# A gain row fetched one group later, and an eviction set behind two weight splits, in a one-layer diffusion block

## The chip, the core and the metric

The kernel runs on one NeuronCore of a Trainium2 chip. Five engines run side by side, each with its own instruction stream: TensorE (PE) multiplies matrices into PSUM; VectorE (DVE) and ScalarE (ACT) work on elements of SBUF and PSUM; GpSimd (POOL) does a few small operations; SyncE (SP) issues most of the DMA transfers, and ACT and POOL issue some. Instructions of one engine start in their order, and engines wait for each other, and for transfers, through semaphores. The metric is the time of one execution in microseconds (us).

## The reference

One layer of a diffusion transformer on 1024 latent tokens and 256 context tokens, width 1024, in float32. With the constants put in, and the parts cut that the change does not touch:

```
sh1, sc1, gt1, sh2, sc2, gt2 = split(silu(c) @ w_mod + b_mod, 6)
h_x = rmsnorm(x, g_pre_mix) * (1 + sc1) + sh1          # the same for the context, with c_ctx
u, q, k, v = split(h @ w_in)                           # latent; of the context only k and v are used
attn = softmax(q k^T / 8 + bias, neighbourhood + all context keys) v
x = x + gt1 * rmsnorm(concat(pool(u), attn) @ w_out, g_post_mix)
h = rmsnorm(x, g_pre_mlp) * (1 + sc2) + sh2
y = square(relu(h @ w_mlp_in)) @ w_mlp_out             # 1024 -> 4096 -> 1024
x = x + gt2 * rmsnorm(y, g_post_mlp)
```

Two quantities matter below. The keys and values of the 256 context tokens come from `w_in`, early in the kernel. The second gate `gt2` is multiplied with the row `g_post_mlp`, and the product scales the MLP's result at the very end.

## The kernel before, in words

**Split products.** Every large product is made of three matmuls: both operands are split into a rounded high part and the rest (`split`, `high_low`), and high x high, high x low and low x high are summed in PSUM (`three`, lines 197 to 200, where most of TensorE's records lie). ACT makes the high part (`high_part`, line 146, or 148 with a factor) and DVE the low part (`low_part`, line 152 or 154). A weight of 128x1024 thus needs one load, one ACT and one DVE instruction before its matmuls can start, the low part being wanted by the second matmul.

**The buffers.** `wraw` has 4 buffers for loaded weights, `whl` has 8 for split ones (so four weights), `act` has 33 pages of 128x1024. They are taken in turn; a new tile waits until the last reader of the old one in that buffer is done.

**The beginning.** Up to line 699 (`startup`) the order on all five engines is the written one. `context_keys(j, ks)` sums the keys of the context in four tiles `pkc0` to `pkc3`, and after the last step of each, ACT copies the PSUM bank into `kc` (line 692). The tiles 2 and 3 come last, each with 24 matmuls over the four split weights `wk0` to `wk3`. Then `difference(0)` runs on DVE, and line 698 splits the four weights of the values, `wv0` to `wv3`, in order, into the buffers that `wk0` to `wk3` leave. The first product with them is `pvc`, the values of the context (line 736), followed by `pv`, those of the latent tokens. The copied keys are read in the attention, much later.

**The MLP's first half** works on 16 blocks of 256 hidden units (`block_pair`), with a fast matrix scheme of seven products (P1 to P7) in place of eight. Its results are stored to DRAM through ACT's DMA queue (`keep`, line 1584). With the last block, the stores are put off and issued at its end by `flush`; the last but one of these is `hdA<-c`. In the last block, the items 0 to 2 of the second half are already prepared (`ahead()` is then `prepare`).

**The MLP's second half** (from line 1808) again holds PE, ACT, DVE and SP to the written order. Its temporary pool `tmp3` is opened where that of the first half, `tmp2`, is closed, so its first tiles lie where the first half's parts lay. The work is a list of items (product, group), each with a load of weights (line 1710, `b`), a load of a stored hidden part (line 1726, `hrA` or `hrS`) and two splits. The first product is P1 with 8 groups, the bank set `pyx`. `group(ps, name, g)` first calls `prepare()`, which sets up the item three places ahead, and then issues the 24 matmuls of group g: so group 0 prepares item 3, group 1 prepares item 4, and so on. The hidden parts of items 0 to 4 of P1 go into `wraw`, later ones into `tmp3`. P1 is followed by P6 and P2 in turns, then P7 and P5, and P4 and P3.

**The second gate.** Its sum over the layer's input, `accb`, is complete in the first half. `mod_gain` loads the row `g_post_mlp` (`gp2`) in four small transfers from SP into the tile `gpb` of `tmp3` (line 243). `mod_gate` sums `accb` over the partitions with four matmul calls (line 236) into the bank `pgb` and multiplies by `gpb` on DVE (line 247). `mod_out` stores the product with four DMAs of POOL (line 253), and in the middle of P6 `gate_page` loads it again, spread over all partitions, as the page that scales the result's rows (line 1847).

Of the kernel before, what the change touches and what calls it, by code (L numbers as in the profile page):

```python
# [11 lines left out]
F32 = mybir.dt.float32  # L12
# [6 lines left out]
P = 128  # L19
D = 1024  # L20
KT = D // P
# [59 lines left out]
def hybrid_block(ctx, tc, x, ctx_in, w_mod, b_mod, gp1, gp2, w_in, pool_w, rpb, w_out, w1, w2, vectors,  # L81
                 mask, edge, out):
    nc = tc.nc
# [97 lines left out]
    def high_low(name, raw, factor=1.0):  # L181
        hi = whl.tile([P, 1024], F32R, tag="hl", name=f"{name}h")
        lo = whl.tile([P, 1024], F32R, tag="hl", name=f"{name}l")
        split(raw, hi, lo, factor)
        return hi, lo
# [7 lines left out]
    def wk(w, k, lo, c, n):  # L193
        return w[k // 2][lo][:, (k % 2) * 512 + c : (k % 2) * 512 + c + n]


    def three(ps, ahi, alo, bhi, blo, first, last, more=False):
        nc.tensor.matmul(ps, ahi, bhi, start=first, stop=False, skip_group_check=more)  # L198
        nc.tensor.matmul(ps, ahi, blo, start=False, stop=False, skip_group_check=more)  # L199
        nc.tensor.matmul(ps, alo, bhi, start=False, stop=last, skip_group_check=more)  # L200
# [39 lines left out]
    def mod_gain(gp, g):  # L240
        quarters = gp.rearrange("(c o f) -> c o f", c=4, o=1)
        for c in range(4):
            nc.sync.dma_start(g[32 * c : 32 * c + 32, :], quarters[c].to_broadcast([32, 256]))
        return g

    def mod_gate(name, acc, g, bank):
        nc.vector.tensor_tensor(acc[:, :256], mod_sums_of(name, acc, bank), g, mul)


    def mod_out(name, acc):  # L250
        gates[name] = dram.tile([1, D], F32, tag=f"g{name}", name=f"g{name}")
        for c in range(4):
            nc.gpsimd.dma_start(gates[name][:, c * 256 : (c + 1) * 256], acc[32 * c : 32 * c + 1, :256])
# [17 lines left out]
    with tc.tile_pool(name="ps1", bufs=6, space=PSUM) as ps1, tc.tile_pool(name="tmp1", bufs=3) as tmp:  # L271

        def bank(name):
            if name[:2] == "pm" or name in ("pxt1_0", "pxt0_2", "pxt1_7", "pct2", "pct3"):
                return lasting(name)
            return ps1.tile([P, 512], F32, tag="mm", name=name)
# [163 lines left out]
        wgt = []  # L440
# [62 lines left out]
        def in_weights(name, raw, kk):  # L503
            return high_low(f"{name}{kk}", raw[kk], 1.0 if kk < 2 else -1.0)
# [62 lines left out]
        hc, wgt = [], []  # L567
# [10 lines left out]
        page_of, raw_v = [], []  # L578
# [66 lines left out]
        def pooled(g, up):  # L645
            w = WINDOWS[g]
            lo, hi = w // 2, w - 1 - w // 2

            bufs = [page(f"sa{g}"), page(f"sb{g}")]
            cur, span, i = up, 1, 0  # L650
            while span < w:
                nxt = bufs[i % 2]
                i += 1
                n = SEQ - 2 * span + 1
                nc.vector.tensor_tensor(nxt[:, :n], cur[:, :n], cur[:, span : span + n], add)
                cur, span = nxt, 2 * span

            ed = tmp.tile([P, 16], F32, tag="ed", name=f"ed{g}", bufs=2)
            nc.vector.reduce_sum(ed[:, 0:1], up[:, 0 : hi + 1], axis=mybir.AxisListType.X)
            for q in range(1, lo):  # L660
                nc.vector.tensor_tensor(ed[:, q : q + 1], ed[:, q - 1 : q], up[:, hi + q : hi + q + 1], add)
            if hi:
                nc.vector.reduce_sum(ed[:, 7 + hi : 8 + hi], up[:, SEQ - 1 - lo : SEQ], axis=mybir.AxisListType.X)
            for q in range(hi - 2, -1, -1):
                t = SEQ - hi + q
                nc.vector.tensor_tensor(ed[:, 8 + q : 9 + q], ed[:, 9 + q : 10 + q], up[:, t - lo : t - lo + 1], add)
            dp = bufs[i % 2]
            nc.vector.scalar_tensor_tensor(dp[:, lo : SEQ - hi], cur[:, : SEQ - w + 1], 1.0 / w,
                                           up[:, lo : SEQ - hi], mul, sub)
            nc.vector.tensor_tensor(ed[:, :lo], ed[:, :lo], edg[:, g, :lo], mul)  # L670
            nc.vector.tensor_tensor(dp[:, :lo], ed[:, :lo], up[:, :lo], sub)
            if hi:
                nc.vector.tensor_tensor(ed[:, 8 : 8 + hi], ed[:, 8 : 8 + hi], edg[:, g, 8 : 8 + hi], mul)
                nc.vector.tensor_tensor(dp[:, SEQ - hi :], ed[:, 8 : 8 + hi], up[:, SEQ - hi :], sub)
            return dp
# [3 lines left out]
        def difference(g):  # L679
            differences[g] = pooled(g, up[g]).rearrange("p (r m c) -> p m r c", r=QR, m=NM)  # L680

        kcp = page("kcT")
        kc = kcp.rearrange("p (j t) -> p j t", j=4)
        pkc = {}

        def context_keys(j, ks):
            if j not in pkc:
                pkc[j] = bank(f"pkc{j}")[:, :CTX]
            for k in ks:
                three(pkc[j], wk(wgt, k, 0, j * P, P), wk(wgt, k, 1, j * P, P), *hc[k], k == 0, k == KT - 1)  # L690
            if k == KT - 1:
                nc.scalar.copy(kc[:, j], pkc[j])

        for js, ks in (((0, 1), range(6)), ((0, 1), (6, 7)), ((2, 3), range(KT))):
            for j in js:
                context_keys(j, ks)
        difference(0)
        wgt = [in_weights("wv", raw_v, kk) for kk in range(KT // 2)]
        startup.close()


# [220 lines left out]
        with in_order(ET.PE, ET.Pool, ET.Activation, ET.DVE, ET.SP) as pooling:  # L922
            banks = {of: [bank(f"p{of}{j}") for j in range(2)] for of in "KQ"}
            use(-1)
            for step, (n, of, j) in enumerate([(n, of, j) for n, of in products for j in range(2)]):
                half_product(n, of, j, banks[of])
                use(step)
                if step in (5, 9, 17):
                    name = {5: "S1", 9: "S4", 17: "S3"}[step]
# [4 lines left out]
                if step in (7, 11):  # L934
                    name = {7: "S4", 11: "S3"}[step]
# [13 lines left out]
    with (  # L949
# [195 lines left out]
        with in_order(ET.PE, ET.Activation, ET.DVE, ET.SP) as projected:  # L1145
# [7 lines left out]
            for i in range(N + 4):  # L1153
# [12 lines left out]
                if i > 3:  # L1166
                    weighed(i - 4)
                    if i % 8 == 3:
                        j = i // 8 - 1
# [3 lines left out]
                if i == 0:  # L1173
                    gain = mod_gain(gp1, att.tile([P, 256], F32, tag="gp", name="gpa"))
# [10 lines left out]
                if 8 < i < N and i % 8 == 7:  # L1185
                    j = i // 8 - 1
# [63 lines left out]
    with tc.tile_pool(name="ps2", bufs=6, space=PSUM) as ps2:  # L1250
# [6 lines left out]
      with ExitStack() as tmp2:  # L1257
        tmp = tmp2.enter_context(tc.tile_pool(name="tmp2", bufs=4))
# [549 lines left out]
        with tc.issue_after(first[ET.PE]), in_order(ET.PE, ET.Activation, ET.DVE, ET.SP):  # L1808
# [5 lines left out]
            tmp = tmp2.enter_context(tc.tile_pool(name="tmp3", bufs=4))  # L1814

            def four(name):
                return [bank(f"{name}_{t}") for t in range(4)]
# [13 lines left out]
            def group(ps, name, g, more=False, last=False):  # L1831
                prepare()
                for t in range(4):
                    token_sums(ps, t, [made.pop((name, g)) if t == 3 else made[name, g]], g == 0 and not more,
                               last or g == NG - 1, more)
# [32 lines left out]


            pg = bank("pgb")  # L1870
            gain = mod_gain(gp2, tmp.tile([P, 256], F32, tag="gp", name="gpb", bufs=1))
            x = four("pyx")
            for g in range(NG):
                if g == 2:
                    mod_gate("b", acc_b[-1], gain, lambda name: pg)
                    mod_out("b", acc_b[-1])
                group(x, "P1", g)
# [84 lines left out]
```

## Time and profile before

| What | Value |
|---|---|
| time, median of 3 runs | 1043.54 us (1043.27 to 1044.52) |
| the profiled execution's own time | 1043.7 us |
| its span, first to last instruction | 1041.9 us |
| TensorE busy | 1021.6 us, 98% of the span |
| DVE busy | 755.9 us, 73% |
| ACT busy | 544.0 us, 52% |
| DMA | 221.63 MB, mean 213 GB/s |
| granted TensorE clock, mean | 0.995 |

How to read the rows that follow. A row of the order in time has: start in us, duration in us, engine, line of the kernel, operation, the tile written, an arrow, the tiles read, the shapes, and in brackets how long the engine had stood before it and for whom. Numbers of tiles are partly left out: `b_3h` is the high part of `b11_3`, `c` is `c21_15`. PEld is TensorE's loading of weights, and SPq, ACTq are the issuing of DMAs. A row of waits has: who waited, for whom, us in total, times, longest. A table by stages has for each window its length, then busy us (and instructions) of PE, PEld, DVE, ACT and POOL, the granted TensorE clock as a share of full, the DMA share and GB/s. A matmul's listed duration is longer than its distance to the next one, since they are pipelined.

### The profile page before, as it was taken

Reading aid. Unit: us, or ns where it says so; the run is one execution under the profiler, and the core shown is the slowest. Engines: PE = TensorE matmul, PEld = TensorE weight load, DVE = VectorE, ACT = ScalarE, POOL = GpSimd, SP = SyncE. Lnnn points to the kernel's source line nnn. Section 1 sums busy time; section 2 is a strip of 40 time slices with the busy share of each in tenths; the row PEclk is TensorE's granted clock in tenths of the full one; section 3 lists DMA queues with packets and bytes.
Section 4 is the critical chain, followed back from the end, with each engine's and each line's share of the span. In section 5 each row is a group of like instructions: output and inputs, shape, how many; then the busy total and the mean of one; then the engine's idle time right before and its main releaser. Section 6 shows DMA issues by size and latency. Waiting matters only on the chain.

```text
span 1041.9 us, 15640 instructions
## 1 busy us (share of the span) xinstructions
PE 1021.6 (98%) x5814; PEld 838.0 (80%) x5814; DVE 755.9 (73%) x1183; ACT 544.0 (52%) x941; POOL 108.3 (10%) x163
## 2 busy tenths in 40 slices
PE   8999999999999999999999999999799999999997
PEld 7788888878877888888888888888588888888885
DVE  5587856878986687879988888755476666547586
ACT  7582254328886657776555554545453334334431
POOL 3011021143311321310000000000000000000001
PEclk9999999999999999999999999999899999999999
DMA  9999699641337966886786667343877666555456
GB/s 345 323 261 325 232 241 303 205 101 43 72 95 190 216 179 194 276 206 204 256 263 210 210 199 239 137 151 132 337 261 282 235 231 223 200 173 194 171 186 207
DMA packets 122908, 221.63 MB, mean 213 GB/s; under 512 B 9424, under 2 KB 55248, under 8 KB 122832
## 3 DMA queue, kind: packets, MB, share of 16 engines
q1 hardware_dynamic: 96608, 170.75, 49.5%
q0 software_dynamic: 9088, 18.92, 9.2%
q10 hardware_dynamic: 17136, 30.97, 8.0%
q8 instruction: 45, 0.74, 0.3%
q14 instruction: 31, 0.25, 0.1%
HBM read 167.63 MB, written 51.92 MB: 211 GB/s over the span
## 4 chain that ended last, share of the span: by engine, by line
PE 92%; ACT 2%; DMA 2%; DVE 2%; issue 1%; SPq 0%; ACTq 0%; DVEq 0%; POOLq 0%
PE pu L449 4%; PE S L977 3%; PE pa L1053 3%; PE pyv L199 3%; PE pyz L199 3%; PE pyv L200 3%; PE pyz L200 3%; PE pyz L198 3%; PE pyv L198 3%; PE phx L198 3%; PE phx L199 3%; PE phx L200 3%; PE phv L198 3%; PE phz L198 3%; PE phv L199 3%; PE phz L199 3%
## 5 line engine op out<-in xcount | busy, mean ns | idle before, releaser
L1000 ACT ACTIVATE sp<-sp,nm 128x640 f32<-128x640 f32 (+1 forms) x64 | 51.4, 803 | 20.0 <-DVE nm L991 19.7
L1563 ACT ACTIVATE c<-c 128x512 f32<-128x512 f32 x48 | 30.3, 632 | 48.1 <-DVE c L1683 24.5
L146 ACT CAST wpS<-S 128x512 fp32r<-128x512 f32 x64 | 38.8, 616 | 28.2 <-PE phv L200 10.1
L198 PE MATMUL phx<-thB,wpA 128*128 128x512 f32 x128 | 50.2, 392 | 0.0
L199 PE MATMUL phx<-tlB,wpA 128*128 128x512 f32 x128 | 49.8, 389 | 0.0
L200 PE MATMUL phx<-thB,wpA 128*128 128x512 f32 x128 | 49.8, 389 | 0.0
L152 DVE TENSOR_TENSOR wpS<-S,wpS 128x512 fp32r<-128x512 f32 x64 | 43.4, 685 | 8.2 <-ACT wpS L146 8.2
L991 DVE CUSTOM_DVE_ANT_0 sp<-S,tab 128x640 f32<-128x640 f32 (+1 forms) x56 | 42.8, 802 | 8.4 <-PE S L977 6.8
L1564 ACT ACTIVATE c<-c 128x512 f32<-128x512 f32 x48 | 30.3, 631 | 14.8 <-DVE sa L1646 12.1
L140 POOL TENSOR_TENSOR ry<-vy,nhalf 128x1 f32<-128x1 f32 x8 | 4.4, 550 | 282.8 <-DVE vy L138 282.8
L198 PEld LDWEIGHTS phx<-thB,wpA 128*128 128x128 f32 x128 | 24.0, 188 | 5.5 <-ACT s L1614 0.5
L977 PE MATMUL S<-kT,q 64*128 64x384 f32 (+1 forms) x128 | 27.8, 495 | 0.3 <-DVE nm L991 0.3
L200 PEld LDWEIGHTS phx<-thB,wpA 128*128 128x128 f32 x128 | 24.0, 188 | 5.1
L199 PEld LDWEIGHTS phx<-tlB,wpA 128*128 128x128 f32 x128 | 24.0, 188 | 4.8
L1053 PE MATMUL pa<-pt,v 128*64 128x128 f32 x352 | 25.9, 279 | 0.8 <-ACT px L1033 0.3
L1038 DVE COPY pt<-T 128x512 f32<-128x512 f32 x32 | 21.9, 686 | 5.5 <-PE T L1019 5.5
L198 PE MATMUL phv<-thT,wpA 128*128 128x512 f32 x64 | 25.0, 391 | 0.0
L198 PE MATMUL phz<-thB,wpS 128*128 128x512 f32 x64 | 25.0, 391 | 0.0
L199 PE MATMUL phv<-tlT,wpA 128*128 128x512 f32 x64 | 24.9, 390 | 0.0
L200 PE MATMUL phz<-thB,wpS 128*128 128x512 f32 x64 | 24.9, 389 | 0.0
L199 PE MATMUL phz<-tlB,wpS 128*128 128x512 f32 x64 | 24.9, 389 | 0.0
L200 PE MATMUL phv<-thT,wpA 128*128 128x512 f32 x64 | 24.9, 389 | 0.0
(1104 smaller groups left out, 3385.1 us busy)
## 6 DMA issues: line engine op xcount, KB each, us to landing
b<-in_w SPq DMA_DIRECT2D x64, 512.0 KB, 4.1
hrS<-hdS SPq DMA_DIRECT2D x32, 512.0 KB, 5.4
hrA<-hdA SPq DMA_DIRECT2D x24, 512.0 KB, 6.4
wm<-in_w_mod SPq DMA_DIRECT2D x16, 512.0 KB, 9.8
wa_0w<-in_w SPq DMA_DIRECT2D x16, 512.0 KB, 4.8
wa_1w<-in_w SPq DMA_DIRECT2D x16, 512.0 KB, 4.3
hdA<-c ACTq DMA_DIRECT2D x32, 256.0 KB, 2.2
hdS<-sa ACTq DMA_DIRECT2D x32, 256.0 KB, 2.4
```

The source lines that it names most:

```text
L146: nc.scalar.copy(hi, src)
L152: nc.vector.tensor_tensor(lo, src, hi.bitcast(F32), sub)
L198: nc.tensor.matmul(ps, ahi, bhi, start=first, stop=False, skip_group_check=more)
L199: nc.tensor.matmul(ps, ahi, blo, start=False, stop=False, skip_group_check=more)
L200: nc.tensor.matmul(ps, alo, bhi, start=False, stop=last, skip_group_check=more)
L449: nc.tensor.matmul(pus[b][j], wk(wgt, k, low, j * P, P), r, start=(k == 0 and n == 0), stop=(k == KT - 1 and n == 2))
L977: nc.tensor.matmul(S[e][:, c0 : c0 + keys.shape[1]], q[hs, cols], keys[hs], start=True, stop=True)
L991: nc.vector.tensor_tensor_reduce(out=to, in0=s, in1=bt, scale=1.0, scalar=BIG, op0=add, op1=ALU.min, accum_out=nm)
L1000: nc.scalar.activation(sp, sp, AF.Exp, bias=least[i, e], scale=-1.0, accum_out=sums[i][:, e : e + 1])
L1053: nc.tensor.matmul(pa[e * HD : (e + 1) * HD, cols], v[:, f : f + HD], turns[i][:, e, c] if c < 4 else fifths[i][:, :, (e + 1) * HD : (e + ...
L1563: nc.scalar.activation(r, src, AF.Relu)
L1564: nc.scalar.activation(r, r, AF.Square)
```

## The change

Two edits. In the beginning, the copy of a context tile's bank into `kc` is taken out of `context_keys` into `context_kept(j)`. For the tiles 0 to 2 it is called where it was. For tile 3 it is called between the split of `wv1` and the split of `wv2`, so that on ACT the order is `wv0h`, `wv1h`, copy, `wv2h`, `wv3h` in place of copy, `wv0h`, `wv1h`, `wv2h`, `wv3h`.

In the MLP's second half, `mod_gain` (the tile `gpb` and its four transfers) is called in the loop over P1's groups, ahead of group 1, in place of ahead of group 0. On SP it thus follows the two loads of the item (P1, 3) and precedes those of (P1, 4). `mod_gate` and `mod_out` are called ahead of group 3 in place of group 2.

```diff
             for k in ks:
                 three(pkc[j], wk(wgt, k, 0, j * P, P), wk(wgt, k, 1, j * P, P), *hc[k], k == 0, k == KT - 1)
-            if k == KT - 1:
-                nc.scalar.copy(kc[:, j], pkc[j])
+
+        def context_kept(j):
+            nc.scalar.copy(kc[:, j], pkc[j])
 
         for js, ks in (((0, 1), range(6)), ((0, 1), (6, 7)), ((2, 3), range(KT))):
             for j in js:
                 context_keys(j, ks)
+                if ks[-1] == KT - 1 and j < 3:
+                    context_kept(j)
         difference(0)
-        wgt = [in_weights("wv", raw_v, kk) for kk in range(KT // 2)]
+        wgt = []
+        for kk in range(KT // 2):
+            wgt.append(in_weights("wv", raw_v, kk))
+            if kk == 1:
+                context_kept(3)
         startup.close()
...
             pg = bank("pgb")
-            gain = mod_gain(gp2, tmp.tile([P, 256], F32, tag="gp", name="gpb", bufs=1))
             x = four("pyx")
             for g in range(NG):
-                if g == 2:
+                if g == 1:
+                    gain = mod_gain(gp2, tmp.tile([P, 256], F32, tag="gp", name="gpb", bufs=1))
+                if g == 3:
                     mod_gate("b", acc_b[-1], gain, lambda name: pg)
                     mod_out("b", acc_b[-1])
                 group(x, "P1", g)
```

## The prediction

> **What bounds the kernel now.** I read the page first: how long the span is, who fills it, and which engine carries the chain that ends last.
>
> ```profile
> span 1041.9 us, 15640 instructions
> PE 1021.6 (98%) x5814; PEld 838.0 (80%) x5814; DVE 755.9 (73%) x1183; ACT 544.0 (52%) x941; POOL 108.3 (10%) x163
> PE 92%; ACT 2%; DMA 2%; DVE 2%; issue 1%; SPq 0%; ACTq 0%; DVEq 0%; POOLq 0%
> ```
>
> TensorE is busy for 98% and carries 92% of the chain, so a change is worth what it gives or takes at the few places where TensorE waits. The second view is therefore the list of waits of TensorE alone, over the whole run, and beside it the longest wait of SP's queue around the largest of them.
>
> ```profile
> PE pyx L198 <- ACT b_3h L146: 5.5, 1, 5.5
> ...
> PE pvc L198 <- ACT wv0h L146: 1.4, 1, 1.4
> ...
> PE pyx L199 <- DVE b_3l L152: 0.7, 1, 0.7
> ```
> ```profile
> SPq L243 <- DMA hdA<-c: 27.4, 1, 27.4
> ```
>
> The reader is to see that two of TensorE's waits lie exactly where the diff is: `pyx` waits for the operands of group 3 of the product P1 (`b_3`), and `pvc` waits for the first weights of the values (`wv0`). SP stood 27.4 us on L243, which is `mod_gain`, until a store at the end of the MLP's first half (`hdA<-c`) had landed. The third view, the order in time on SP, shows what stood behind that wait; ACT and DVE show what came of it; PE shows the price.
>
> ```profile
> 705.51 0.34 SPq L1726 DMA_DIRECT2D hrA<-hdA  x1
> 733.46 1.73 SPq L243 DMA_DIRECT2D gpb<-in_gp  x4
> 735.30 0.38 SPq L1710 DMA_DIRECT2D b<-in_w  x1
> 735.73 0.47 SPq L1726 DMA_DIRECT2D hrA<-hdA  x1
> ```
> ```profile
> 731.08 0.49 ACTq L1584 DMA_DIRECT2D hdS<-sb  x1
> 740.66 1.04 ACT L146 CAST hhA_3h<-hrA 128x1024 fp32r<-128x1024 f32 x1 [10.87 <-DMA hrA<-hdA]
> 741.61 1.04 ACT L146 CAST b_3h<-b 128x1024 fp32r<-128x1024 f32 x1
> ```
> ```profile
> 742.88 1.22 DVE L152 TENSOR_TENSOR b_3l<-b,b_3h 128x1024 fp32r<-128x1024 f32 x1
> ```
> ```profile
> 736.79 0.39 PE L200 MATMUL pyx<-b_2h,hhA_2l 128*128 128x512 f32 x1
> 742.70 0.79 PE L198 MATMUL pyx<-b_3h,hhA_3h 128*128 128x512 f32 x1 [5.52 <-ACT b_3h L146]
> 744.15 0.80 PE L199 MATMUL pyx<-b_3l,hhA_3h 128*128 128x512 f32 x1 [0.66 <-DVE b_3l L152]
> 751.23 0.39 PE L198 MATMUL pyx<-b_4h,hhA_4h 128*128 128x512 f32 x1
> 756.67 0.39 PE L198 MATMUL pyx<-b_5h,hhA_5h 128*128 128x512 f32 x1
> ```
>
> SP issued nothing between the loads of item 2 (705.51) and the gain row (733.46); the loads of item 3 came last in that line (735.30, 735.73). A group unhindered is 24 matmuls in 756.67 - 751.23 = 5.44 us, 0.227 us each. Group 2 began its last matmul at 736.79, so group 3 could have begun at 737.02 and group 4 at 742.46; group 4 began at 751.23. The place costs 8.77 us. Not all of that is waiting: after it TensorE ran at half clock for some 5 us, as the table by stages shows (behind the window's length and the busy times of PE, PEld, DVE, ACT and POOL stands PEclk).
>
> ```profile
> 89.50:91.00 1.50, 1.47 (x6) 1.24 (x7) 1.50 (x2) 1.50 (x2) 1.20 (x2) 1.00 1.01 370
> 742.70:747.70 5.00, 4.34 (x9) 3.13 (x10) 4.62 (x6) 3.60 (x4) 0.33 (x1) 0.50 1.04 400
> ```
>
> **The gain row behind item 3.** The four issues of `mod_gain` move on SP from ahead of the loads of (P1, 3) to behind them, ahead of those of (P1, 4). On SP they are passed by two issues, `b11_3` and `hrA11_3`; POOL's queue is passed by nothing. Both loads then depend on their buffers only. The hidden part goes into a weight buffer whose last reader is the split of block 15's `wa15_1`, and `b11_3` into the page next in turn: `b_1` waited for block 15's `phx` and `b_2` for its `phy`, so the next follows `phz`.
>
> ```profile
> 707.11 0.68 DVE L154 SCALAR_TENSOR_TENSOR wpA<-wa_1w,wpA 128x512 fp32r<-128x512 f32 x1
> 708.79 0.39 PE L200 MATMUL phz<-thT,wpS 128*128 128x512 f32 x1
> ```
> ```profile
> DMA to landing us min/median/max: 4.9/8.3/11.5
> ```
>
> So both are free by 709.2, and even with the slowest landing of a hidden part in this stage (the row above, `hrA` from 730 to 760: 11.5 us) they are there by some 722. ACT does its work in the written order, so the split of item 3 stands behind the last store it issues (731.08 + 0.49 = 731.57): `hhA_3h` and `b_3h` end at 733.6, and `b_3l`, which ends 2.5 us after ACT begins `b_3h` (744.10 against 741.61), at 735.0. Group 3 wants them at 737.02. Its wait goes to nothing, with 2 us in hand.
>
> What is late next is item 4. The gain row still waits for the same store, so SP still issues it at 733.46 and then, in item 3's old places, `b11_4` and `hrA11_4`. I give item 4 the times that item 3 has now: `b_4h` done at 742.65, `b_4l` at 744.10. Group 4 would begin at 742.46. Its first matmul waits to 742.70, its second to 744.15, and 23 more at 0.227 us put group 5 at 749.36. Now it begins at 756.67. This edit gives 7.31 us: the stall falls from 8.77 to 749.36 - (742.46 + 5.44) = 1.46 us. Ends of this term: 8.77 if item 4's split were also in time, and 5.4 if the clock falls in group 4 as it now does in group 3 (23 matmuls now take 751.23 - 744.15 = 7.08 us and not 5.21, so 1.87 us). I take full clock, because 1.5 us of waiting is nearest to the 1.41 us at `pvc`, after which the window from 89.50 shows 1.00, and far from 5.52 us, after which the one from 742.70 shows 0.50. The Trainium skill, "TensorE: Matmul & The Clock Gate", section on the HAM clock gate, states that about one idle window of 3.4 us halves the clock and that the window runs free; by that the sum stays 7.31, and it would be 5.4 only if item 4 came some 2 us later than I put it. The two clock readings here agree with it; the limit itself no row here shows.
>
> **What gives this gain back later.** Items 5 to 7 follow item 4 by one place earlier than now. The tightest cover is at the start of P6, whose first weights are ready at 759.22 + 1.22 = 760.4.
>
> ```profile
> 759.22 1.22 DVE L152 TENSOR_TENSOR t_0l<-t,t_0h 128x1024 fp32r<-128x1024 f32 x1
> ```
> ```profile
> 772.99 0.39 PE L198 MATMUL pyy<-t_0h,hhS_0h 128*128 128x512 f32 x1
> ```
>
> That is 12.6 us ahead of its use; 7.3 us less leaves 5.3 us. I cost it at nothing; without the cover, each late us is one us. TensorE has no other wait after 745.
>
> **The gate one group later.** Eight short matmuls (0.64 us) and one DVE product move from group 2 to group 3 and cost the same there. The product stays between two splits, and its result is wanted only when the gate's page is read, long after.
>
> ```profile
> 730.87 0.64 PE L236 MATMUL pgb<-accb,ones 128*32 128x256 f32 x8
> ```
> ```profile
> L1847 DVE TENSOR_TENSOR row<-pyx,Gb x4: 678/682/691, 858.9 to 861.0; 128x512 f32<-128x512 f32 x4
> ```
>
> POOL's four stores of it and the page's load lie in the 100 us and more between group 3 and 858.9: nothing.
>
> **The context's last eviction behind two splits.** ACT now stands on `pkc` of tile 3 while `wv0w` has already landed (issued at 74.8, 7.8 us to landing, so at 82.6, by the last rows below).
>
> ```profile
> 85.56 0.28 PE L199 MATMUL pkc<-hc,wk0h 128*128 128x256 f32 x1
> 87.84 0.28 PE L200 MATMUL pkc<-hc,wk3l 128*128 128x256 f32 x1
> 89.53 0.50 PE L198 MATMUL pvc<-wv0h,hc 128*128 128x512 f32 x1 [1.41 <-ACT wv0h L146]
> ```
> ```profile
> 88.16 0.37 ACT L692 COPY kcT<-pkc 128x256 f32<-128x256 f32 x1 [2.50 <-PE pkc L200]
> 88.43 1.05 ACT L146 CAST wv0h<-wv0w 128x1024 fp32r<-128x1024 f32 x1
> ```
> ```profile
> L178 SPq DMA_DIRECT2D wv0w<-in_w_in x1: 384/384/384, 74.8 to 74.8; - x1
> ...
> DMA to landing us min/median/max: 7.8/7.8/7.8
> ```
>
> `wv0h` takes over the buffer of `wk0h`, whose last reader in the fourth context tile ends at 85.84. So `wv0h` runs 85.9 to 87.0 and its low part on DVE, which is idle here, to 88.2; `wv1h` to 88.0; then the eviction, at 88.16 as now; `wv2h` follows at 88.4. TensorE could go on at 87.96 (context matmuls come every 0.12 us) and goes on at 89.53: 1.57 us, of which I take 1.5, since the second matmul then meets `wv0l` within 0.1 us. Ends: 1.6 and 0. Zero, if the following stage, turns the head start into waits of its own; but ACT and DVE start on these splits 2.5 us sooner too (85.9 against 88.43). The evicted keys are read only in the attention.
>
> **The sum.** 7.31 + 1.5 = 8.8 us. The profiled execution took 1043.7 us for its span of 1041.9, the median of the runs is 1043.54: 1043.54 - 8.8 = 1034.7 us.
>
> **Rivals.**
> 1. *Only the MLP edit pays* (the values' stage eats 1.5 us): 1036.2. For it: DVE is full further on (third number of busy time):
>
> ```profile
> 102.00:110.00 8.00, 8.00 (x37) 6.63 (x36) 8.00 (x12) 0.84 (x2) 0.17 (x1) 1.00 0.30 105
> ```
>
> Against: TensorE is full there too and has no wait.
> 2. *The clock falls in group 4*: 1034.7 + 1.87 = 1036.6. It needs item 4 about 2 us later; the spread of landings allows it.
> 3. *Item 3's loads are not issued early*, because a buffer is held to the end of block 15 or the queue's order is another: then group 3 waits as now and only 1.5 us come: 1042.0.
> 4. *The stall is handed on whole and grows* (the other side): item 4 now stands behind the gain row alone. Landings of hidden parts run from 4.9 to 11.5 us. Item 4's took 4.9 in my sum; at 11.5 the stall is 1.46 + 6.6 + 1.87 = 9.9 us, and with 1.5 from the first edit the time is 1043.2, no change. It is slower by over 0.2% once the landing passes 1.5 + 2.1 + 8.77 - 1.46 - 1.87 + 4.9 = 13.9 us; at 15 us it gives 1046.7. The long landings now come when the engines are full, and the first pair after the gap has the short ones.
>
> **How the numbers follow.** Forecast 0.72, rivals 0.12, 0.08, 0.04 and 0.04. The forecast alone spans 1033.2 (both terms at their upper ends, 8.77 + 1.57) to 1036; with rivals 1 and 2 the range goes to 1038.0 (both of them, 1038.1). About 0.2%, 2.1 us, is what a measurement of this kernel can tell from no change. Faster 0.92 (the forecast, 1 and 2), same 0.04 (rival 3), slower 0.04.
>
> **What the changed profile would show.** Right: SP's `b` and `hrA` of item 3 before 715; the gain row still some 27 us on `hdA<-c`; no wait of PE on `b_3h`, one of about 1 us on `b_4l`; PEclk at full in the slice where it now reads 8; `wv0h` at about 86, no wait of `pvc`. All later times shift by 1.5 us. Wrong: a wait on `b_4h` of several us, or waits in the values' stage that add to 1.5 us. The prediction falls if item 3's loads still follow the gain row.

## The result, and the profile after

The changed kernel takes 1035.06 us (median of 5 runs, 1034.35 to 1035.89); the kernel before took 1044.52 us on the same chip (1043.27 to 1045.25). The ratio is 0.9912, with a 95% interval of 0.9898 to 0.9927: 9.2 us less, between 7.6 and 10.7. The forecast was 1034.7 us, 8.8 us less. That the times lie within 0.4 us of each other is partly luck: the forecast was counted from a time before of 1043.54 us (3 runs), and over the 5 runs it is 1.0 us more; the forecast gain of 8.8 us lies within the measured interval.

In the changed kernel the lines behind `context_kept` carry a number 7 higher than before: 1717 and 1733 are the loads `b` and `hrA` that were 1710 and 1726.

The page of the changed kernel, with its span and the busy times:

```profile
span 1034.1 us, 15642 instructions
PE 1019.2 (99%) x5814; PEld 837.0 (81%) x5814; DVE 755.7 (73%) x1183; ACT 544.0 (53%) x941; POOL 108.3 (10%) x163
```

The work is the same; the span is shorter by 7.8 us. TensorE is listed as 2.4 us less busy for the same 5814 matmuls: the first matmul of group 3 at half clock was listed with 0.79 us, and none there is now above 0.50.

TensorE's waits in the changed kernel (who waited, for whom; us in total, times, longest):

```profile
PE pu L449 <- ACT hx L208: 1.6, 1, 1.6
...
PE pyx L199 <- DVE b_4l L152: 1.0, 1, 1.0
```

The waits of `pyx` on `b_3h` (5.5 us) and `b_3l` (0.7 us) and that of `pvc` on `wv0h` (1.4 us) are gone. One of 1.0 us on `b_4l` has come. The wait at `pu` stood at 0.4 us in the profiled execution before. That matmul starts at 24.49 us in place of 23.21, ahead of anything that the change touches, and the beginning stays 1.3 us later up to the values' stage. So spans of two executions can differ by 1.3 us for no reason of the change, and I measure between two places behind it.

**The values' stage** in the changed kernel, on ACT, DVE and TensorE:

```profile
86.56 0.37 ACT L693 COPY kcT<-pkc 128x256 f32<-128x256 f32 x1 [2.51 <-PE pkc L200]
87.16 1.05 ACT L146 CAST wv0h<-wv0w 128x1024 fp32r<-128x1024 f32 x1 [0.23 <-PE pkc L199]
88.11 1.04 ACT L146 CAST wv1h<-wv1w 128x1024 fp32r<-128x1024 f32 x1
89.44 0.37 ACT L693 COPY kcT<-pkc 128x256 f32<-128x256 f32 x1 [0.29 <-PE pkc L200]
```
```profile
88.24 1.23 DVE L152 TENSOR_TENSOR wv0l<-wv0w,wv0h 128x1024 fp32r<-128x1024 f32 x1 [4.41 <-ACT wv0h L146]
```
```profile
89.12 0.28 PE L200 MATMUL pkc<-hc,wk3l 128*128 128x256 f32 x1
89.24 0.39 PE L198 MATMUL pvc<-wv0h,hc 128*128 128x512 f32 x1
89.52 0.50 PE L199 MATMUL pvc<-wv0l,hc 128*128 128x512 f32 x1
```

The two splits lie between two copies of `pkc`, and `pvc` follows the last `pkc` matmul after 0.12 us, at the distance of two matmuls without any wait. Before it followed after 89.53 - 87.84 = 1.69 us: 1.57 us gained. The eviction runs to 89.81 and nobody waits for it.

**The first groups of P1**, in the changed kernel: SP, the longest waits of SP's queue there, ACT, DVE, and TensorE.

```profile
705.14 0.34 SPq L1733 DMA_DIRECT2D hrA<-hdA  x1
710.30 0.37 SPq L1717 DMA_DIRECT2D b<-in_w  x1
719.06 0.34 SPq L1733 DMA_DIRECT2D hrA<-hdA  x1
732.94 1.73 SPq L243 DMA_DIRECT2D gpb<-in_gp  x4
734.77 0.38 SPq L1717 DMA_DIRECT2D b<-in_w  x1
735.20 0.47 SPq L1733 DMA_DIRECT2D hrA<-hdA  x1
```
```profile
SPq L243 <- DMA hdA<-c: 13.3, 1, 13.3
...
SPq L1733 <- DMA hdA<-r: 8.3, 1, 8.3
```
```profile
731.11 1.05 ACT L146 CAST hhA_3h<-hrA 128x1024 fp32r<-128x1024 f32 x1 [1.82 <-DMA hdS<-sa]
732.07 1.05 ACT L146 CAST b_3h<-b 128x1024 fp32r<-128x1024 f32 x1
739.99 1.05 ACT L146 CAST hhA_4h<-hrA 128x1024 fp32r<-128x1024 f32 x1 [6.88 <-DMA hrA<-hdA]
```
```profile
742.22 1.22 DVE L152 TENSOR_TENSOR b_4l<-b,b_4h 128x1024 fp32r<-128x1024 f32 x1
```
```profile
736.37 0.50 PE L198 MATMUL pyx<-b_3h,hhA_3h 128*128 128x512 f32 x1
742.04 0.49 PE L198 MATMUL pyx<-b_4h,hhA_4h 128*128 128x512 f32 x1
743.49 0.50 PE L199 MATMUL pyx<-b_4l,hhA_4h 128*128 128x512 f32 x1 [0.95 <-DVE b_4l L152]
748.85 0.39 PE L198 MATMUL pyx<-b_5h,hhA_5h 128*128 128x512 f32 x1
```

The gain row still goes out only when the same store has landed (732.94, against 733.46 before). It stands for 13.3 us and not for the 27 us forecast, because SP now reaches it only behind item 3's loads. These go out at 710.30 and 719.06, and ACT splits item 3 as soon as it has issued its last store, at 731.11. Group 3 starts without a wait. Item 4 has taken item 3's old places (734.77 and 735.20), and its low part comes at 743.44, when group 4 has already done its first matmul. Groups 3 and 4 take 748.85 - 736.37 = 12.48 us for 2 x 5.44 = 10.88 us of unhindered work, so 1.60 us are left of the 8.77 us that the place cost.

The table by stages for group 4 (window's length, busy us and counts of PE, PEld, DVE, ACT, POOL, then PEclk, DMA share, GB/s):

```profile
741.00:743.00 2.00, 1.53 (x6) 0.76 (x5) 1.93 (x2) 0.99 (x2) 0.00 (x0) 1.00 1.04 409
743.00:746.00 3.00, 2.51 (x11) 2.08 (x12) 1.50 (x2) 2.00 (x2) 0.00 (x0) 1.00 1.04 400
```

The clock stays full. From the last `pkc` matmul to the first matmul of group 5 it was 756.67 - 87.84 = 668.83 us and is 748.85 - 89.12 = 659.73 us: 9.10 us less, of which 1.57 lie at `pvc`, 7.17 (8.77 - 1.60) in groups 3 and 4, and 0.36 are spread over the 647 us between (runs with the same order there differ by as much: 647.1 to 647.6 us). Less the 1.3 us of the later beginning this is the 7.8 us between the spans.

### The profile page after: what moved, and what is told of

Same layout as the page of the kernel before. It is cut to its first block, busy times and chain, and to the rows that moved or that the text cites. A ratio compares the mean times of both kernels' runs of the same rounds, so it can differ in the third digit from the quotient of the medians.

```text
span 1034.1 us, 15642 instructions
## 1 busy us (share of the span) xinstructions
PE 1019.2 (99%) x5814; PEld 837.0 (81%) x5814; DVE 755.7 (73%) x1183; ACT 544.0 (53%) x941; POOL 108.3 (10%) x163
## 4 chain that ended last, share of the span: by engine, by line
PE 91%; DMA 3%; ACT 2%; DVE 1%; issue 1%; SPq 1%; ACTq 0%; DVEq 0%; POOLq 0%
PE pu L449 4%; PE S L984 3%; PE pa L1060 3%; PE pyv L200 3%; PE pyv L199 3%; PE pyz L200 3%; PE pyz L199 3%; PE pyv L198 3%; PE pyz L198 3%; PE phx L198 3%; PE phx L200 3%; PE phx L199 3%; PE phv L198 3%; PE phz L198 3%; PE phv L199 3%; PE phz L199 3%
```

## The experiments

The prediction's theory: what counts is the order on SP. Item 3's loads stood behind the waiting gain row; whatever takes the row out of their way gives some 7.3 us, and the eviction gives 1.5 us beside it. The questions put to it: do the two edits really add up, or does one of them carry all; does the gate's new place count; is the cause the order on the queue or the buffer that makes the row wait; and how much of the price was the clock. Each run is compared with the kernel before on its own chip (medians 1044.03 to 1044.36 us).

### One edit at a time

```diff
-            if k == KT - 1:
-                nc.scalar.copy(kc[:, j], pkc[j])
...
+            wgt.append(in_weights("wv", raw_v, kk))
+            if kk == 1:
+                context_kept(3)
```

> Only the first edit: the context's last eviction behind two splits, the MLP as before. My theory: TensorE's 1.4 us at pvc goes and nothing takes it back, so 1.5 us less than before (a ratio of 0.9986), and the wait on b_3h stays at 5.5 us. Rival: the head start is lost in the values' stage or the attention, 0 us. The profile tells them apart better than the times: the distance from the last context matmul to the first matmul of P1's group 3 should be 1.5 us shorter by my theory, and equal by the rival.

Measured: 1042.30 us, ratio 0.9984 (0.9975 to 0.9992), 1.7 us less. TensorE's longest wait in it, and the end of the keys:

```profile
PE pyx L198 <- ACT b_3h L146: 5.3, 1, 5.3
```
```profile
87.75 0.28 PE L200 MATMUL pkc<-hc,wk3l 128*128 128x256 f32 x1
87.87 0.39 PE L198 MATMUL pvc<-wv0h,hc 128*128 128x512 f32 x1
```

`pvc` follows at once here too. The distance that the expectation named as the test, from the last `pkc` matmul to the first of group 3, is 741.40 - 87.75 = 653.65 us against 742.70 - 87.84 = 654.86: 1.2 us shorter, so the stages behind do not take the 1.57 us back. The wait on `b_3h` stays (0.2 us shorter).

```diff
-            gain = mod_gain(gp2, tmp.tile([P, 256], F32, tag="gp", name="gpb", bufs=1))
...
-                if g == 2:
+                if g == 1:
+                    gain = mod_gain(gp2, tmp.tile([P, 256], F32, tag="gp", name="gpb", bufs=1))
+                if g == 3:
```

> Only the second edit: gain row ahead of group 1, gate ahead of group 3, the beginning as before. My theory: 7.3 us less than before (0.9930), one wait of PE on b_4l of about 1 us, full clock, and the 1.4 us at pvc stay. Rival: the two edits help each other and do not add up; then this run and the run with the first edit alone give together clearly less or more than the 9.2 us of both (0.9912).

Measured: 1036.16 us, ratio 0.9922 (0.9909 to 0.9935), 8.1 us less. The waits of TensorE in it are those of the changed kernel plus the old one at `pvc`. The product of the two ratios, 0.9984 x 0.9922 = 0.9906, is the changed kernel's 0.9912 within its interval: the edits add up.

### The gate's place alone

```diff
-                if g == 2:
+                if g == 3:
                     mod_gate("b", acc_b[-1], gain, lambda name: pg)
```

> The kernel before, with only the gate's sum, product and stores moved from ahead of group 2 to ahead of group 3; the row stays ahead of group 0. My theory: 0 us (1.000), at most the 0.7 us of its eight short matmuls, which now fall into the stall of group 3 in place of ahead of it: then 0.7 us less (0.9993). Rival: DVE's product, one split later, holds a split that TensorE waits for: slower by up to 0.4 us.

Measured: 1044.01 us, ratio 0.9999 (0.9990 to 1.0008). Moving the sum and its stores by one group changes nothing that these runs can tell (1 us either way); the second edit's gain belongs to the row.

### The row in a buffer of its own

The gain row waits for a late store because its tile lies where the first half's parts lay. Here it has a tile that nothing else uses; its place in the order is that of before.

```diff
-            gain = mod_gain(gp2, tmp.tile([P, 256], F32, tag="gp", name="gpb", bufs=1))
+            gain = mod_gain(gp2, cst("gpb", [P, 256]))
```

> The kernel before, with the gain row's tile in a buffer of its own in place of one in the pool that the first half leaves; order of all issues as before. Theory A (the store holds SP only through the buffer): the row is issued at about 706, items 3 and 4 load early, groups 3 and 4 do not wait: 8.8 us less than before (0.9916). Theory B (the completion semaphores: each transfer of SP and ACT takes the next of eight in turn and waits for its last user, which now would be the stores at the end of the first half): the last of the row's four waits for the store of 729.2, item 3's two loads for those of 729.5 and 730.0, so they are issued at about 732, 3.4 us sooner than now; group 3 then waits about 2.3 us for b_3h at full clock, and the run gains 3.4 + 1.9 = 5.2 us (0.9950), or 3.4 if the clock falls all the same (0.9967).

Measured: 1042.65 us, ratio 0.9987 (0.9977 to 0.9996), 1.4 us less. SP's waits in this run, and its order in time:

```profile
SPq L243 <- DMA hdS<-sa: 10.9, 1, 10.9
SPq L243 <- DMA hdA<-r: 8.4, 1, 8.4
SPq L243 <- DMA b<-in_w: 4.8, 1, 4.8
```
```profile
712.54 20.74 SPq L243 DMA_DIRECT2D gpb<-in_gp  x4
734.41 0.36 SPq L1726 DMA_DIRECT2D hrA<-hdA  x1
```

The row no longer waits for `hdA<-c`, and its first piece goes out at 712.54. But its four pieces, issued over 20.74 us, now wait for transfers that have nothing to do with its buffer: two stores of the last block and a load of weights. In the program that the kernel is compiled to, SP's and ACT's transfers take eight completion semaphores in turn (the trace names the semaphore of each transfer, and these eight numbers come round), and a transfer must wait until the one that used its semaphore before has landed. So the order held SP nearly as long, and item 3's loads were only about 3 us earlier against the last stores. Of these 3 us, 1.2 went in the landing: this `hrA` takes 6.1 us from issue to landing, against 4.9 before. The wait on `b_3h` went from 5.5 to 3.7 us. The expectation had the semaphores right and the gain too large (3.4 to 5.2 us): beside the landing, half clock lasted further into the work, so that groups 3 and 4 took 757.13 - 742.62 = 14.51 us, against 13.97 before. The profiled execution is also a slow one of the twelve, which run from 1041.25 to 1045.39 us (it took 1044.15). The buffer was the condition that ended last, and the next one stood close behind it.

### The row on another queue

```diff
-    def mod_gain(gp, g):
+    def mod_gain(gp, g, queue=None):
...
-            nc.sync.dma_start(g[32 * c : 32 * c + 32, :], quarters[c].to_broadcast([32, 256]))
+            (queue or nc.sync).dma_start(g[32 * c : 32 * c + 32, :], quarters[c].to_broadcast([32, 256]))
...
-            gain = mod_gain(gp2, tmp.tile([P, 256], F32, tag="gp", name="gpb", bufs=1))
+            gain = mod_gain(gp2, tmp.tile([P, 256], F32, tag="gp", name="gpb", bufs=1), nc.gpsimd)
```

> The kernel before, with the gain row's four transfers issued by POOL in place of SP; the tile, its buffer and its wait for the stores stay. If SP's order is what costs (what stands behind the waiting row), items 3 and 4 now load ahead of the stores' end as in the run with the row two groups later: no wait on b_3h or b_4l, 8.8 us less than before (0.9916). If the row's own late arrival or the number of transfers at this place were the cost, it would stay at 1.000.

Measured: 1035.25 us, ratio 0.9914 (0.9901 to 0.9928), 9.0 us less. No wait of TensorE on any `b` is left. The row's buffer, its store to wait for and its place in the written order are those of before; only the queue differs, and with it the semaphores that tell of its landing. On POOL the row goes out at 734.97, when `hdA<-c` has landed (734.05), and keeps nobody. The bracket in its row counts how long POOL had no other work, and names not the store but the last instruction to end before it:

```profile
720.05 0.34 SPq L1726 DMA_DIRECT2D hrA<-hdA  x1
...
731.84 0.34 SPq L1726 DMA_DIRECT2D hrA<-hdA  x1
```
```profile
734.97 1.99 POOL L243 DMA_DIRECT2D gpb<-in_gp  x4 [136.63 <-DVE hhA_3l L152]
```

These are the hidden parts of item 3 (720.05) and item 4 (731.84). This shows the prediction's theory: the row's wait costs nothing by itself, what stands behind it on SP costs. With the first edit added:

> The first edit together with the gain row on POOL's queue at its old place. My theory: the two pay in different stages and add up, 0.9984 x 0.9914 = 0.9898 of before, as with the row two groups later (0.9896). Rival: with the row's transfers on POOL the product of the gate comes later on DVE and holds the splits of item 5 (2.2 us of waiting there with the row on POOL), which without the slack of the first edit reaches TensorE: a wait on b_5 and 0.991.

Measured: 1034.22 us, ratio 0.9902 (0.9889 to 0.9916), 10.2 us less. TensorE waits for no `b` here, so the rival (a wait on `b_5`) did not come.

### The row two groups later

Both edits, with the row ahead of group 2 and the gate ahead of group 4, so that the loads of items 3 and 4 both precede the row.

```diff
-                if g == 1:
+                if g == 2:
                     gain = mod_gain(gp2, tmp.tile([P, 256], F32, tag="gp", name="gpb", bufs=1))
-                if g == 3:
+                if g == 4:
```

> Both edits, with the gain row one group later still: ahead of group 2, behind items 3 and 4; the gate ahead of group 4. My theory: the wait on b_4l (1.0 us and what goes with it, 1.5 us in my sum) goes too, since item 5, which now stands behind the row, has one group more: 1.4 us less than the changed kernel, about 10.5 us less than before (0.9899). Rival: the wait only moves to b_5, or hrA of item 4 is held by the stores until 731 and comes too late: no gain over the changed kernel (0.9912).

Measured: 1033.33 us, ratio 0.9896 (0.9883 to 0.9908), 10.9 us less: 1.7 us below the changed kernel, about the 1.60 us that groups 3 and 4 still lost there. The two intervals overlap, but the traces agree: from the last `pkc` matmul to the first of group 6 it is 663.71 us here and 665.17 in the changed kernel. Item 4's hidden part goes out ahead of the row:

```profile
729.60 0.34 SPq L1733 DMA_DIRECT2D hrA<-hdA  x1
731.96 2.80 SPq L243 DMA_DIRECT2D gpb<-in_gp  x4
```
```profile
739.00:745.00 6.00, 6.00 (x32) 4.39 (x32) 2.39 (x3) 3.12 (x4) 0.00 (x0) 1.00 1.03 398
```

In the window where groups 3 and 4 meet, TensorE is busy for 6.00 of 6.00 us. No wait on a `b` is left; item 5 and the later ones are in time. This is the shortest time of the kernels tried, though not apart from that of the first edit with the row on POOL (0.9902) by more than their intervals.

### One split ahead of the eviction

The changed kernel, with the eviction behind the first split alone.

```diff
-            if kk == 1:
+            if kk == 0:
                 context_kept(3)
```

> The changed kernel, with the context's last eviction behind the first split of the values' weights only. ACT then waits for the last context matmul before wv1h, which ends about 1.5 us later than with both ahead; wv1l ends 1.3 us after TensorE wants it. By my theory a wait of 1.2 us on wv1l at pvc takes the place of the one on wv0h: about 1.2 us more than the changed kernel (0.9923 of before), unless TensorE is given other matmuls of wv0h ahead of it, and then nothing is lost (0.9912).

Measured: 1034.93 us, ratio 0.9910 (0.9897 to 0.9924), no different from the changed kernel. The second weight is split later, but TensorE does not wait for it:

```profile
90.02 1.23 DVE L152 TENSOR_TENSOR wv1l<-wv1w,wv1h 128x1024 fp32r<-128x1024 f32 x1 [1.33 <-ACT wv1h L146]
```
```profile
90.72 0.40 PE L200 MATMUL pvc<-wv0h,hc 128*128 128x512 f32 x1
...
91.41 0.39 PE L199 MATMUL pvc<-wv1l,hc 128*128 128x512 f32 x1
```

Behind the startup the order is no longer the written one, and the matmuls with `wv0` for further tiles have been placed ahead of those with `wv1l`. So one split ahead is enough, and the 1.57 us are the price of `wv0h` alone.

### What the halved clock costs

Of the 8.77 us, the prediction put 1.87 us down to the clock, which fell while TensorE waited. To keep TensorE busy in that gap, 36 transposes of the identity were added to the kernel before, ahead of group 3; their result is not used.

```diff
+                if g == 3:
+                    for _ in range(36):
+                        nc.tensor.transpose(pg[:, 256:384], ident, ident)
                 group(x, "P1", g)
```

> The kernel before, with 36 idle transposes of 128x128 on TensorE ahead of group 3 (into an unused part of the bank pgb): about 4.5 us of the 5.5 us in which it waits are filled, at 0.126 us each. The wait itself is not shortened. If the 1.87 us that I put to the halved clock are the clock's, PEclk stays at 1.00 and group 3 runs at 0.227 us a matmul: 1.9 us less than before (0.9982). If group 3 is slow for another reason (its operands, the full DMA engines), nothing changes (1.000).

Measured: 1050.66 us, ratio 1.0065 (1.0053 to 1.0078). TensorE's longest wait, its last matmul before it, and a window of half a microsecond in it:

```profile
PE pgb L1879 <- DVE accb L247: 9.7, 1, 9.7
```
```profile
736.57 0.39 PE L200 MATMUL pyx<-b_2h,hhA_2l 128*128 128x512 f32 x1
```
```profile
739.00:739.50 0.50, 0.00 (x0) 0.00 (x0) 0.00 (x0) 0.00 (x0) 0.00 (x0) 0.55 0.91 369
```

The expectation of 1.9 us less was missed, because `pg` is also the bank that the gate's product reads on DVE, and that product stands in DVE's order behind the late row; so the transposes began only 9.7 us later. The run still shows how soon the clock can fall: the window with 0.55 is at full clock for its first 0.05 us and at half for the rest, so the fall is at 739.05, 2.1 us after the end of the last matmul (736.96). In the next run they have a bank of their own:

```diff
+            fill = bank("fill")
...
+                        nc.tensor.transpose(fill[:, :128], ident, ident)
```

> The kernel before, with the 36 idle transposes ahead of group 3 written to a bank of their own, so that they wait for nothing: they fill about 4.5 us of the 5.5 us of TensorE's wait, which itself is not shortened. If the 1.87 us that I put to the halved clock are the clock's, PEclk stays at 1.00, group 3 runs at 0.227 us a matmul, and the run takes 1.9 us less than before (0.9982). If group 3 is slow for another reason, such as the full DMA engines, nothing changes (1.000).

Measured: 1045.48 us, ratio 1.0008 (0.9999 to 1.0017). TensorE and ACT in order of time, and a window of half a microsecond:

```profile
737.83 4.09 PE L1880 MATMUL fill<-ident 128*128 128x128 f32 x36
745.11 0.80 PE L198 MATMUL pyx<-b_3h,hhA_3h 128*128 128x512 f32 x1 [3.19 <-ACT b_3h L146]
```
```profile
743.07 1.05 ACT L146 CAST hhA_3h<-hrA 128x1024 fp32r<-128x1024 f32 x1 [12.43 <-DMA hrA<-hdA]
```
```profile
744.50:745.00 0.50, 0.00 (x0) 0.00 (x0) 0.50 (x1) 0.50 (x1) 0.00 (x0) 0.77 1.00 401
```

The transposes ended at 741.92, but item 3's hidden part landed 6.5 us after its issue at 736.55 in place of 4.9, so 3.2 us of waiting were left, and the clock fell in them after all, at 744.77, 2.9 us after the last transpose. This profiled execution is the slowest of eleven. Over them the mean granted clock goes from 0.995 to 0.998 and the time from 1046.81 down to 1043.11 us, so in some the clock probably fell for a shorter time or not at all; as their waits are not on record, the run does not measure what the clock alone costs.

The kernel before itself answers the expectation's rival (full DMA engines). Its clock record turns from half to full at 747.88, in the middle of group 3. Two windows, one at half clock and one behind the turn:

```profile
744.20:747.80 3.60, 3.60 (x9) 2.86 (x10) 3.33 (x4) 2.80 (x4) 0.43 (x1) 0.50 1.03 398
748.80:751.20 2.40, 2.40 (x12) 2.00 (x11) 2.09 (x3) 1.96 (x2) 0.49 (x2) 1.00 1.02 390
```

The DMA engines are as full in both. The matmuls start 0.427 us apart from 744.74 to 747.73, and 0.227 us from 748.74 on. So the slow part of group 3 goes with the clock and not with the transfers. The 1.87 us are what this costs over 23 matmuls, a reading of one trace and not a difference of times.

## Why the prediction was right, point by point

The time came at 1035.06 us for 1034.7. The steps, one by one:

**The gain row behind item 3: 7.31 us forecast, 7.17 us in groups 3 and 4.** The mechanism is shown by two different edits that take the row out of the loads' way: moved behind them (8.1 us), or to POOL's queue (9.0 us). The gain of the row alone has an interval of 6.8 to 9.5 us, which holds the forecast. The remaining stall was put at 1.46 us and is 1.60 us, on the low part of item 4, as said; the clock stayed full after it, as it does after the 1.41 us at `pvc`. The prediction named the Trainium skill's page "TensorE: Matmul & The Clock Gate", section on the HAM clock gate, for an idle window of about 3.4 us that runs free. The traces agree with the free-running window: between its first and its last change in a run, the clock keeps a state for a whole number of stretches of 3.413 us, in all twelve profiles (in the kernel before 733.87 us at full, 215 of them, then 6.83 us at half, 2 of them, then 290.13 us at full, 85 of them). They do not bear out that the window must be idle throughout. In the kernel before, whose row is below, the fall came at 741.05, 3.9 us after the last matmul (737.18); in the run with the first edit alone after 3.5 us, with the row in its own buffer after 3.1, in the two with transposes after 2.9 and 2.1, and in the run with the gate alone after 2.2 us. In the run with 2.1 us, TensorE was busy for the first 1.32 of the 3.41 us that end at the fall. So a gap need not reach 3.4 us to lose the clock; what counts is how much of one window it fills, and the place of the windows differs from execution to execution. The waits of 1.0 and 1.4 us did not lose it.

```profile
741.00:741.50 0.50, 0.00 (x0) 0.00 (x0) 0.00 (x0) 0.50 (x1) 0.00 (x0) 0.55 1.03 414
```

**One step of it was wrong: "Both loads then depend on their buffers only".** `b` of item 3 went out at 710.30, but `hrA` at 719.06, not before 715. Both stood for the previous user of their completion semaphore, `b` for the load of the `b` before it (landed at 710.22), `hrA` 8.3 us for the store `hdA<-r` (landed at 719.00). The prediction did not consider this condition, and no tile in the code shows it. It did no harm because ACT, as forecast, was the later condition: it reached the split of item 3 only at 731.11, and `hrA` landed at 722.26. That the turn gave `hrA` a store so early was luck. Had the turn of the eight semaphores fallen on one of the last stores, something like rival 3 (no early load, 1042.0 us) would be expected. That order was not run; the nearest is the run with the row in its own buffer, where item 3's loads had to wait for such stores (1042.65 us, without the eviction's edit).

**The later items.** Forecast: nothing comes late behind item 4, with 5.3 us of cover left at the start of P6. Measured: no wait, and more cover, since the split itself came earlier too. DVE and TensorE in the changed kernel:

```profile
756.13 1.23 DVE L152 TENSOR_TENSOR t_0l<-t,t_0h 128x1024 fp32r<-128x1024 f32 x1
```
```profile
765.17 0.39 PE L198 MATMUL pyy<-t_0h,hhS_0h 128*128 128x512 f32 x1
```

757.36 to 765.17 is 7.8 us. The step held the split at its old time, which was too careful by 2.5 us.

**The gate one group later: nothing forecast, nothing measured** (0.9999).

**The eviction behind two splits: 1.5 us forecast, 1.57 us in the trace** and 1.7 us (0.8 to 2.6) in the run of this edit alone. `wv0l` was in time for the second matmul. That two splits were needed was not claimed, and is not so.

**The rivals.** Rival 1 (the values' stage takes the gain back) fell with the first edit run alone. Rival 2 (clock falls in group 4) fell with the windows of the changed kernel at 1.00, though with less in hand than the prediction's 2 us: item 4 some 1.2 us later would have made a gap of 2.1 us, which is enough where it lies in one window. Rival 4 (the stall handed on and grown) came only in its harmless form: the stall was handed on to item 4, whose hidden part landed 4.8 us after its issue, near the 4.9 us that were assumed.

## What to carry to other kernels

A queue that issues in order makes one waiting transfer as expensive as everything behind it. When the list of waits shows an issue standing for long, look first not at what it waits for but at who is queued behind it: move it behind the urgent loads or to an idle queue, and go on as long as an urgent load is left behind it (here one group more gave another 1.7 us). Giving the waiting transfer a free buffer may not help, since the next condition, here the completion semaphores taken in turn, can stand right behind.

## What was not expected of the hardware

- The clock's fall came 2.1 to 3.9 us after the last matmul, in six traces of nearly the same place. The moments lie on a grid of 3.413 us that runs on through each execution; a stretch of it in which TensorE was busy for up to 1.32 us was followed by half clock (the run with transposes in `pg`). At `pvc`, the wait of 1.4 us was followed by full clock.
- In this program a transfer can wait for an older one with which it shares no tile. SP stood 8.3 us (changed kernel) and 8.4 and 10.9 us (row in its own buffer) on such stores.
- The first 512 KB load of a hidden part behind the gap took 4.5 to 4.9 us from issue to landing in six traces, where it followed the last store's issue by 4.6 us. It took 6.1 us when it was issued 1.6 us behind the last of them (734.41 against 732.85), and 6.5 us in the run with the transposes, where its distance to the stores was 4.6 us. With the row on POOL, item 4's hidden part was issued 0.3 us behind the last store and took 5.1 us. So the distance to the stores does not explain it; the cause is open.
- The start of the kernel varies by 1.3 us between executions, ahead of TensorE's first long matmuls, also among kernels with the same beginning. Why was not looked for.
